# Conditioning columns from small fp32 products with the summed rows as stationary operand, in place of broadcast sums and their diagonal

## The chip, the cores and the metric

The kernel runs on one core of one Trainium2 chip. Its engines are TensorE (PE in the profile; its weight loads are shown apart as PEld), VectorE (DVE), ScalarE (ACT), GpSimd (POOL) and SyncE (SP, which here issues nearly all DMAs). The metric is the time of one execution in device microseconds, the median of three runs.

## The reference, cut to what matters

One layer for 256 tokens of width 2048 (D), with a conditioning vector `c` for the whole sequence. Each of three sublayers is modulated by columns of `ada`, and closed by a gate and a layer norm:

```python
ada = (silu(c) @ w_ada + b_ada)[:, None, :]          # 2048 -> 9 * 2048
sh1, sc1, g1, sh2, sc2, g2, sh3, sc3, g3 = split(ada, 9, axis=-1)
h = swiglu(layernorm(x) * (1 + sc1) + sh1, ffn1_w_in, ffn1_w_out)       # width 5632
x = layernorm(ALPHA * x + 0.5 * (1 + g1) * h, ln1_g, ln1_b)
h = token_mixer(layernorm(x) * (1 + sc2) + sh2, ..., w_in, ..., w_out)  # 8 FoX heads, 4 mLSTM heads
x = layernorm(ALPHA * x + (1 + g2) * h, ln2_g, ln2_b)
h = swiglu(layernorm(x) * (1 + sc3) + sh3, ffn2_w_in, ffn2_w_out)
x = layernorm(ALPHA * x + 0.5 * (1 + g3) * h, ln3_g, ln3_b)
```

The change concerns `sh2, sc2` (vectors 3 and 4 of the nine) and `sh3, sc3` (vectors 6 and 7): 2 x 2 x 2048 numbers.

## The kernel before, in words

**The products.** Every large product is made of three products in fp32r, a rounded fp32: `split` (L141) has ACT cast a tile to its rounded part `hi`, and DVE subtract that to get the rest `lo`; `mm3` (L368 to L371) then adds hi by hi, lo by hi and hi by lo into one accumulator of 128 x 256 or 128 x 512. One TensorE instruction is one such product with a stationary operand of 128 x 128. The weights arrive in DMAs of 1 MB, issued by SP at L344 into the three `raw` buffers; their halves are split into six `hi` and six `lo` buffers, so at most three loads are ahead of their use, and a load waits for its `raw` buffer.

**The stages**, in the order of the program: layer norm of `x`; FFN1 into the hidden rows (`gu_f`, L369 to L371), FFN1 out (`o_f`); a norm; the mixer's input products (`b_fv`, `b_mv`: values of the two kinds of heads, and others), the heads, and its output product (`o_mx`, from the weights `raw_mxo`, and the head outputs `yhi`, `ylo`); a norm; FFN2 in (`gu_f`) and out (`o_f`); the last norm.

**The conditioning.** `silu(c)` stands in `csil`, one column for each of 16 blocks of 128 rows of `w_ada`. `ada_acc` (L153) has DVE multiply a block of 128 rows by its column and add it to `acc`, 128 x 1024: sixteen such steps leave in `acc` a sum over blocks, and what is still to be summed is the 128 partitions. Each step is fed by a DMA of 512 KB on the SP queue (L179), into two `araw` buffers; so such a DMA waits for the accumulation two steps before, and whatever stands behind it on the SP queue waits too. `ada_gate` (L194) makes a gate, `ada_pair(v, js)` (L173) makes shift and scale together as columns: 512 features of vector `v` and 512 of `v+1` for each block `j`. In the text below a block is called 3_0 to 3_3 or 6_0 to 6_3 after its `v` and `j`; the eight blocks fill `scsh[:, v:v+2, 4j:4j+4]`, with feature 128q+p of the block in partition p and column q.

To sum over partitions, `ada_pair` before the change splits each 512-wide half of `acc` into `ahi` and `alo` and multiplies both by a stationary matrix of ones (`onesr`, in the trace `trir`): the sum `bc`, 128 x 512, then has every feature in every partition. DVE multiplies it by the identity (`dg`, L188) and reduces each 128 columns (L190), which leaves the diagonals: the columns wanted. Another DVE step adds the bias (L192).

**What sets the order.** The conditioning runs beside the big products as a generator, `ada_queue` (L218): gate of vector 2, blocks 3_0 to 3_3, 6_0 and 6_1, gate 5, blocks 6_2 and 6_3, gate 8. At fixed places of the program `pump(rate)` (L229) adds a rate (1.25 to 0.6 steps) to what is owed, and advances the generator by whole steps. A `yield PAUSE` ends the pump at once, with the debt kept: it gives the engines time between two dependent steps, and the generator makes the steps owed at the next pump. Within this, the framework's scheduler places the instructions on each engine, by their dependences and the buffers. `need` (L239) drains the generator to a point. Small sums use the PSUM pool of three `aux` buffers. Small tiles of the conditioning share the pool `ap` with one buffer per tag: `acc`, `ahi`, `alo`.

**A form that both kernels have.** For vectors 0 and 1, `first_columns` (L708) already makes columns with plain fp32 products: stationary `acc[:, v, qs]` of 128 x 128, moving `ones[:, 0:1]`, one result column (L716, tiles `cp` and `cq`).

Of the kernel before, what the change touches and what calls it, by code (L numbers as in the profile page):

```python
# [7 lines left out]
F32 = mybir.dt.float32  # L8
F32R = mybir.dt.float32r
AF = mybir.ActivationFunctionType  # L10
ALU = mybir.AluOpType
AX = mybir.AxisListType
PSUM = bass.MemoryType.PSUM

P = 128
T = 256
D = 2048
KD = D // P
# [14 lines left out]
def layer_kernel(  # L33
# [8 lines left out]
    V, S, G_, PE, SP = nc.vector, nc.scalar, nc.gpsimd, nc.tensor, nc.sync  # L42
# [16 lines left out]
    ap = ctx.enter_context(tc.tile_pool(name="ap", bufs=1))  # L59
# [7 lines left out]
    def aux_tile(name):  # L67
        return pa.tile([P, 512], F32, tag="aux", name=name)


    ident = cst.tile([P, P], F32, name="ident")
    G_.memset(ident, 0.0)
    G_.affine_select(out=ident, in_=ident, compare_op=ALU.not_equal, fill=1.0, base=0,
                     pattern=[[-1, P]], channel_multiplier=1)
    tri = ap.tile([P, 2 * P], F32, tag="ahi", name="tri")
    G_.memset(tri, 1.0)
    G_.affine_select(out=tri[:, :P], in_=tri[:, :P], compare_op=ALU.is_ge, fill=0.0, base=0,
                     pattern=[[1, P]], channel_multiplier=-1)
# [3 lines left out]
    ones, onesr = triu1[:, P:], trir[:, P:]  # L82


    crow = ap.tile([KD, P], F32, tag="alo", name="crow")
    SP.dma_start(crow, c[0].rearrange("(k p) -> k p", p=P))
    res = cst.tile([P, 2, D], F32, name="res")
    for a in range(2):
# [10 lines left out]
    G_.memset(mhalf, -0.5)  # L99

    def load_bcol():
        brow = ap.tile([72, 2, P], F32, tag="ahi", name="brow")
        SP.dma_start(brow, b_ada[0].rearrange("(h r p) -> r h p", h=2, p=P))
        bps = aux_tile("bps")
        for i in range(2):
            PE.transpose(bps[:, i * 72:(i + 1) * 72], brow[:, i, :], ident[:72, :72])
        V.tensor_copy(bcol.rearrange("p v k -> p (v k)"), bps[:, :144])
        for v in (1, 4, 7):
            V.tensor_scalar_add(bcol[:, v, :], bcol[:, v, :], 1.0)
# [31 lines left out]
    def split(src, hi, lo):  # L141
        S.copy(hi, src)  # L142
        return V.tensor_tensor(out=lo, in0=src, in1=hi.bitcast(F32), op=ALU.subtract)  # L143
# [15 lines left out]


    def ada_split(acc, tag):
        ahi = ap.tile([P, 512], F32R, tag="ahi", name=f"ahi{tag}")
        alo = ap.tile([P, 512], F32R, tag="alo", name=f"alo{tag}")
        split(acc, ahi, alo)
        return ahi, alo

    def ada_sum(parts, tag):
        bc = aux_tile(f"bc{tag}")
        for i in range(2):
            PE.matmul(bc, onesr, parts[i], start=i == 0, stop=i == 1)  # L170
        return bc

    def ada_pair(v, js):  # L173
        for j in js:
            src = pair_cols(v, j)
            acc = ap.tile([P, 2, 512], F32, tag="acc", name=f"acc{v}_{j}")
            for k in range(KD):
                raw = ap.tile([P, 2, 512], F32, tag="araw", bufs=2, name=f"ar{v}_{j}_{k}")
                SP.dma_start(raw, src[k * P:(k + 1) * P])  # L179
                ada_acc(acc, raw, k)  # L180
                yield
            for i in range(2):
                parts = ada_split(acc[:, i, :], f"{v}_{j}_{i}")
                for _ in range(2):
                    yield PAUSE
                bc = ada_sum(parts, f"{v}_{j}_{i}")
                dg = ap.tile([P, 4, P], F32, tag="alo", name=f"dg{v}_{j}_{i}")
                V.tensor_tensor(out=dg, in0=bc.rearrange("p (a b) -> p a b", b=P),  # L188
                                in1=ident.unsqueeze(1).to_broadcast([P, 4, P]), op=ALU.mult)
                V.tensor_reduce(out=scsh[:, v + i, j * 4:(j + 1) * 4], in_=dg, axis=AX.X, op=ALU.add)  # L190
            cs = scsh[:, v:v + 2, j * 4:(j + 1) * 4]
            V.tensor_tensor(out=cs, in0=cs, in1=bcol[:, v:v + 2, j * 4:(j + 1) * 4], op=ALU.add)  # L192

    def ada_gate(v, s):  # L194
        for j in range(2):
# [20 lines left out]
    PAUSE = 1  # L216
# [1260 lines left out]
```

## Time and profile before

| | us |
|---|---|
| median of three runs | 1932.42 (1932.11 to 1934.88) |
| profiled execution | 1936.38 |
| its span in the trace | 1934.7 |
| busy in the span: PE | 1895.6 (98%), 13085 instructions |
| PEld | 1722.5 (89%) |
| DVE | 1485.6 (77%) |
| ACT | 954.6 (49%) |
| POOL | 56.3 (3%) |
| bytes moved by DMA | 510.90 MB, mean 264 GB/s |
| granted TensorE clock, mean | 0.994 |

The profile is one execution; the span runs from its first to its last recorded instruction, and the run's own time is 1.7 us above it. A busy share of 98% is an average over stages: where an engine with such a share is never idle, every instruction added to it lengthens the run, while in a stage where it waits, the instruction that releases it counts. The profile's view by windows gives busy times stage by stage, the view of waits says in which stretch an engine stood idle and which instruction of which other engine ended that.

### The profile page before, as it was taken

The page shows a single profiled execution, that of the slowest core. Times are in us where ns is not written, and L with a number is a line of the kernel's source. Part 1 is how long each engine was busy: PE and PEld are TensorE (multiplying, and loading weights), DVE is VectorE, ACT ScalarE, POOL GpSimd, SP SyncE. Part 2 cuts the span into 40 slices and gives each one's busy share as a digit, 9 for nine tenths or more (in the row PEclk, how much of TensorE's full clock was granted, in tenths as well). Part 3 has the DMA queues.
Part 4 walks back from the last instruction along what each step waited for, and adds up shares of the span by engine and source line. Part 5 has one row for each costly group of instructions (what it writes and reads, how often), then busy time and mean ns, then how long its engine had stood idle before and what let it go on. Part 6 is the DMA issues. An engine that isn't in the chain of part 4 may idle for free.

```text
span 1934.7 us, 32285 instructions
## 1 busy us (share of the span) xinstructions
PE 1895.6 (98%) x13085; PEld 1722.5 (89%) x13085; DVE 1485.6 (77%) x1838; ACT 954.6 (49%) x1352; POOL 56.3 (3%) x82
## 2 busy tenths in 40 slices
PE   6999999999999999999999999999999999999997
PEld 3999999999988888698998786999999999988886
DVE  5779989777889898888888789777766665555776
ACT  3554454443454555845755545555444444444552
POOL 1111100000000000100000000000000000000000
PEclk8999999999999999999999999999999999999999
DMA  9978969899998786498888884997776776655552
GB/s 352 372 260 317 324 222 318 296 309 312 304 337 311 264 302 222 155 325 297 274 293 285 278 289 173 300 307 247 253 252 227 261 238 196 238 185 188 194 196 87
DMA packets 295709, 510.90 MB, mean 264 GB/s; under 512 B 10850, under 2 KB 158722, under 8 KB 294536
## 3 DMA queue, kind: packets, MB, share of 16 engines
q1 hardware_dynamic: 287784, 480.53, 73.3%
q0 software_dynamic: 7776, 28.32, 4.2%
q8 instruction: 102, 1.67, 0.3%
q14 instruction: 47, 0.39, 0.1%
HBM read 506.71 MB, written 2.10 MB: 263 GB/s over the span
## 4 chain that ended last, share of the span: by engine, by line
PE 78%; issue 11%; DMA 6%; DVE 3%; ACT 1%; POOL 0%; SPq 0%; DVEq 0%; ACTq 0%; POOLq 0%
PE gu_f L369 8%; PE gu_f L371 8%; PE gu_f L370 8%; PE o_f L369 8%; PE o_f L371 8%; PE o_f L370 8%; PE s L369 4%; PE s L371 4%; PE s L370 4%; DMA ar<-in_w_ada_dram 3%; PE fh L369 2%; PE fh L371 2%; PE fh L370 2%; PE fs L369 1%; PE fs L370 1%
## 5 line engine op out<-in xcount | busy, mean ns | idle before, releaser
L157 DVE SCALAR_TENSOR_TENSOR acc<-ar,csil,acc 128x1024 f32<-128x1024 f32 x242 | 308.0, 1274 | 84.4 <-DMA ar<-in_w_ada_dram 82.8
L369 PE MATMUL s<-xhi_f,hi_s 128*128 128x256 f32 x768 | 213.2, 278 | 1.1 <-ACT hT1a L825 1.1
L370 PE MATMUL s<-xlo_f,hi_s 128*128 128x256 f32 x768 | 213.1, 277 | 0.0
L371 PE MATMUL s<-xhi_f,lo_s 128*128 128x256 f32 x768 | 212.8, 277 | 0.0
L371 PE MATMUL gu_f<-xhi_f,lo_f2i 128*128 128x256 f32 x768 | 212.0, 276 | 0.0
L369 PE MATMUL gu_f<-xhi_f,hi_f2i 128*128 128x256 f32 x768 | 212.0, 276 | 0.0
L370 PE MATMUL gu_f<-xlo_f,hi_f2i 128*128 128x256 f32 x768 | 212.0, 276 | 0.0
L143 DVE TENSOR_TENSOR lo_f2i<-raw_f2i,hi_f2i 128x1024 fp32r<-128x1024 f32 x96 | 117.5, 1224 | 88.3 <-ACT hi_f2i L142 88.2
L371 PE MATMUL gu_f<-xhi_f,lo_f1i 128*128 128x256 f32 x640 | 176.7, 276 | 0.0
L369 PE MATMUL gu_f<-xhi_f,hi_f1i 128*128 128x256 f32 x640 | 176.7, 276 | 0.0
L370 PE MATMUL gu_f<-xlo_f,hi_f1i 128*128 128x256 f32 x640 | 176.7, 276 | 0.0
L142 ACT CAST hi_f2i<-raw_f2i 128x1024 fp32r<-128x1024 f32 x96 | 100.8, 1050 | 135.1 <-PE gu_f L370 124.3
L142 ACT CAST hi_s<-raw_s 128x1024 fp32r<-128x1024 f32 x96 | 100.3, 1052 | 130.1 <-PE s L370 83.7
L369 PEld LDWEIGHTS s<-xhi_f,hi_s 128*128 128x128 f32 x768 | 144.7, 189 | 1.3 <-ACT hT1a L825 1.3
L370 PEld LDWEIGHTS s<-xlo_f,hi_s 128*128 128x128 f32 x768 | 144.9, 189 | 0.2 <-DVE xlo_f L300 0.2
L371 PEld LDWEIGHTS s<-xhi_f,lo_s 128*128 128x128 f32 x768 | 144.9, 189 | 0.0
L370 PEld LDWEIGHTS gu_f<-xlo_f,hi_f2i 128*128 128x128 f32 x768 | 144.1, 188 | 0.2
L369 PEld LDWEIGHTS gu_f<-xhi_f,hi_f2i 128*128 128x128 f32 x768 | 144.1, 188 | 0.2
L371 PEld LDWEIGHTS gu_f<-xhi_f,lo_f2i 128*128 128x128 f32 x768 | 144.1, 188 | 0.0
L143 DVE TENSOR_TENSOR lo_f2o<-raw_f2o,hi_f2o 128x1024 fp32r<-128x1024 f32 x88 | 107.8, 1225 | 44.9 <-ACT hi_f2o L142 44.8
L143 DVE TENSOR_TENSOR lo_s<-raw_s,hi_s 128x1024 fp32r<-128x1024 f32 x96 | 115.8, 1223 | 29.0 <-ACT hi_s L142 29.0
L369 PE MATMUL o_f<-hi_f2o,hh 128*128 128x512 f32 x344 | 135.2, 393 | 0.0
(502 smaller groups left out, 5383.9 us busy)
## 6 DMA issues: line engine op xcount, KB each, us to landing
ar<-in_w_ada_dram SPq DMA_DIRECT2D x227, 512.0 KB, 5.6
raw_f2i<-in_ffn_w_in_dram SPq DMA_DIRECT2D x48, 1024.0 KB, 5.2
raw_s<-in_ffn_w_in_dram SPq DMA_DIRECT2D x47, 1024.0 KB, 7.4
raw_f1o<-in_ffn_w_out_dram SPq DMA_DIRECT2D x44, 1024.0 KB, 6.7
raw_f2o<-in_ffn_w_out_dram SPq DMA_DIRECT2D x44, 1024.0 KB, 5.0
raw_f1i<-in_ffn_w_in_dram SPq DMA_DIRECT2D x40, 1024.0 KB, 7.8
ar<-in_w_ada_dram POOLq DMA_DIRECT2D x48, 512.0 KB, 6.9
raw_mxo<-in_w_out_dram SPq DMA_DIRECT2D x16, 1024.0 KB, 6.3
```

The lines of the kernel that those rows point to most:

```text
L142: S.copy(hi, src)
L143: return V.tensor_tensor(out=lo, in0=src, in1=hi.bitcast(F32), op=ALU.subtract)
L157: V.scalar_tensor_tensor(out=acc, in0=raw, scalar=csil[:, k:k + 1], in1=acc, op0=ALU.mult, op1=ALU.add)
L369: PE.matmul(o, ah, bh, start=start, stop=False)
L370: PE.matmul(o, ah, bl, start=False, stop=False)
L371: PE.matmul(o, al, bh, start=False, stop=stop)
```

## The change

Each block's `acc` is copied once by ACT into `rows`, 128 x 1024. After two pauses, eight products in plain fp32 take 128 columns each of `rows` as the stationary operand and one column of ones as the moving one; each leaves the sums of 128 features as one column of `cp` in PSUM, 128 x 8 for the block. One DVE step adds the bias and writes `scsh`. The two splits, the four products with the matrix of ones, the multiplication by the identity, the two reductions and two of the four pauses are gone. In the gates, which keep the matrix of ones, the split parts now lie in one tile `as`; `tri`, `brow` and `crow`, used at the start, take other tags.

```diff
--- before.py
+++ after.py
@@ -72,7 +72,7 @@
     G_.memset(ident, 0.0)
     G_.affine_select(out=ident, in_=ident, compare_op=ALU.not_equal, fill=1.0, base=0,
                      pattern=[[-1, P]], channel_multiplier=1)
-    tri = ap.tile([P, 2 * P], F32, tag="ahi", name="tri")
+    tri = ap.tile([P, 2 * P], F32, tag="as", name="tri")
     G_.memset(tri, 1.0)
     G_.affine_select(out=tri[:, :P], in_=tri[:, :P], compare_op=ALU.is_ge, fill=0.0, base=0,
                      pattern=[[1, P]], channel_multiplier=-1)
@@ -82,7 +82,7 @@
     ones, onesr = triu1[:, P:], trir[:, P:]
 
 
-    crow = ap.tile([KD, P], F32, tag="alo", name="crow")
+    crow = ap.tile([KD, P], F32, tag="acc", name="crow")
     SP.dma_start(crow, c[0].rearrange("(k p) -> k p", p=P))
     res = cst.tile([P, 2, D], F32, name="res")
     for a in range(2):
@@ -99,7 +99,7 @@
     G_.memset(mhalf, -0.5)
 
     def load_bcol():
-        brow = ap.tile([72, 2, P], F32, tag="ahi", name="brow")
+        brow = ap.tile([72, 2, P], F32, tag="as", name="brow")
         SP.dma_start(brow, b_ada[0].rearrange("(h r p) -> r h p", h=2, p=P))
         bps = aux_tile("bps")
         for i in range(2):
@@ -159,10 +159,9 @@
 
 
     def ada_split(acc, tag):
-        ahi = ap.tile([P, 512], F32R, tag="ahi", name=f"ahi{tag}")
-        alo = ap.tile([P, 512], F32R, tag="alo", name=f"alo{tag}")
-        split(acc, ahi, alo)
-        return ahi, alo
+        parts = ap.tile([P, 2, 512], F32R, tag="as", name=f"as{tag}")
+        split(acc, parts[:, 0, :], parts[:, 1, :])
+        return parts[:, 0, :], parts[:, 1, :]
 
     def ada_sum(parts, tag):
         bc = aux_tile(f"bc{tag}")
@@ -179,17 +178,16 @@
                 SP.dma_start(raw, src[k * P:(k + 1) * P])
                 ada_acc(acc, raw, k)
                 yield
+            rows = ap.tile([P, 2, 512], F32, tag="as", name=f"rows{v}_{j}")
+            S.copy(rows, acc)
+            for _ in range(2):
+                yield PAUSE
+            cp = aux_tile(f"cc{v}_{j}")[:, :8].rearrange("p (v k) -> p v k", v=2)
             for i in range(2):
-                parts = ada_split(acc[:, i, :], f"{v}_{j}_{i}")
-                for _ in range(2):
-                    yield PAUSE
-                bc = ada_sum(parts, f"{v}_{j}_{i}")
-                dg = ap.tile([P, 4, P], F32, tag="alo", name=f"dg{v}_{j}_{i}")
-                V.tensor_tensor(out=dg, in0=bc.rearrange("p (a b) -> p a b", b=P),
-                                in1=ident.unsqueeze(1).to_broadcast([P, 4, P]), op=ALU.mult)
-                V.tensor_reduce(out=scsh[:, v + i, j * 4:(j + 1) * 4], in_=dg, axis=AX.X, op=ALU.add)
-            cs = scsh[:, v:v + 2, j * 4:(j + 1) * 4]
-            V.tensor_tensor(out=cs, in0=cs, in1=bcol[:, v:v + 2, j * 4:(j + 1) * 4], op=ALU.add)
+                for q in range(4):
+                    PE.matmul(cp[:, i, q:q + 1], rows[:, i, q * P:(q + 1) * P], ones[:, 0:1], start=True, stop=True)
+            V.tensor_tensor(out=scsh[:, v:v + 2, j * 4:(j + 1) * 4], in0=cp, in1=bcol[:, v:v + 2, j * 4:(j + 1) * 4],
+                            op=ALU.add)
 
     def ada_gate(v, s):
         for j in range(2):
```

The line numbers of the changed kernel are lower by two behind the first edit, so L369 to L371 of before are L367 to L369 there.

**On PE**, in FFN1 in, around block 3_0. The `gu_f` rows are the large products; `bc` are the products with the matrix of ones (`trir`), the second half's a hundred instructions after the first's. Before:

```order
L371 MATMUL gu_f120_1_5700<-xhi_f1_124,lo_f1i20_0_11_5790 128x256
L170 MATMUL bc3_0_0_5817<-ahi3_0_0_5689,trir_87 128x512
L170 MATMUL bc3_0_0_5817<-alo3_0_0_5690,trir_87 128x512
L369 MATMUL gu_f120_0_5699<-xhi_f1_124,hi_f1i20_1_00_5829 128x256
...
L371 MATMUL gu_f120_1_5700<-xhi_f1_124,lo_f1i20_1_11_5916 128x256
L170 MATMUL bc3_0_1_5943<-ahi3_0_1_5823,trir_87 128x512
L170 MATMUL bc3_0_1_5943<-alo3_0_1_5824,trir_87 128x512
L369 MATMUL gu_f121_0_5975<-xhi_f1_124,hi_f1i21_0_00_5979 128x256
```

Now, with `rows` as the stationary operand:

```order
L368 MATMUL gu_f120_1_5694<-xlo_f1_125,hi_f1i20_0_11_5783 128x256
L369 MATMUL gu_f120_1_5694<-xhi_f1_124,lo_f1i20_0_11_5784 128x256
L188 MATMUL cc3_0_5811<-trir_87,rows3_0_5685 128x1 x8
L367 MATMUL gu_f120_0_5693<-xhi_f1_124,hi_f1i20_1_00_5836 128x256
L368 MATMUL gu_f120_0_5693<-xlo_f1_125,hi_f1i20_1_00_5836 128x256
```

Two pairs at two places have become eight in one place, between two large products as before.

**On SP**, from the mixer's products for the values (`raw_mv512_3` is the last weight load of one column range, `raw_mv0` and `raw_m0a`, `raw_m0b` follow; `ar6_1_k` is step k of block 6_1). Before:

```order
L344 DMA raw_mv512_3_9271<-in_w_in_dram 128x4x520
L344 DMA raw_mv0_0_9351<-in_w_in_dram 128x4x512
L344 DMA raw_mv0_1_9401<-in_w_in_dram 128x4x512
L179 DMA ar6_1_0_9492<-in_w_ada_dram 128x2x512
L344 DMA raw_mv0_2_9450<-in_w_in_dram 128x4x512
L179 DMA ar6_1_1_9495<-in_w_ada_dram 128x2x512
L344 DMA raw_mv0_3_9526<-in_w_in_dram 128x4x512
L344 DMA raw_m0a_0_9572<-in_w_in_dram 128x8x256
L344 DMA raw_m0a_1_9633<-in_w_in_dram 128x8x256
L179 DMA ar6_1_2_9498<-in_w_ada_dram 128x2x512
L344 DMA raw_m0b_0_9694<-in_w_in_dram 128x8x256
L179 DMA ar6_1_3_9501<-in_w_ada_dram 128x2x512
```

Now:

```order
L342 DMA raw_mv512_3_9252<-in_w_in_dram 128x4x520
L178 DMA ar6_1_0_9240<-in_w_ada_dram 128x2x512
L178 DMA ar6_1_1_9243<-in_w_ada_dram 128x2x512
L342 DMA raw_mv0_0_9335<-in_w_in_dram 128x4x512
L178 DMA ar6_1_2_9246<-in_w_ada_dram 128x2x512
L178 DMA ar6_1_3_9249<-in_w_ada_dram 128x2x512
L342 DMA raw_mv0_1_9381<-in_w_in_dram 128x4x512
L178 DMA ar6_1_4_9318<-in_w_ada_dram 128x2x512
L178 DMA ar6_1_5_9369<-in_w_ada_dram 128x2x512
L342 DMA raw_mv0_2_9433<-in_w_in_dram 128x4x512
L178 DMA ar6_1_6_9372<-in_w_ada_dram 128x2x512
L178 DMA ar6_1_7_9415<-in_w_ada_dram 128x2x512
```

The pauses of block 6_0 stood here: up to `raw_m0a_1` two steps of the conditioning went between the loads, and now there are two behind each load.

**On SP**, at the end of the mixer's output product, where `raw_mxo1536_*` are the last weight loads and `ar6_2_k`, `ar6_3_k` steps of the blocks 6_2 and 6_3. Before:

```order
L344 DMA raw_mxo1536_1_12272<-in_w_out_dram 128x4x512
L179 DMA ar6_2_10_12101<-in_w_ada_dram 128x2x512
L179 DMA ar6_2_11_12142<-in_w_ada_dram 128x2x512
L179 DMA ar6_2_12_12181<-in_w_ada_dram 128x2x512
L179 DMA ar6_2_13_12184<-in_w_ada_dram 128x2x512
L344 DMA raw_mxo1536_2_12282<-in_w_out_dram 128x4x512
L179 DMA ar6_2_14_12223<-in_w_ada_dram 128x2x512
L179 DMA ar6_2_15_12262<-in_w_ada_dram 128x2x512
L344 DMA raw_mxo1536_3_12294<-in_w_out_dram 128x4x512
L179 DMA ar6_3_0_13025<-in_w_ada_dram 128x2x512
L344 DMA raw_mxo1536_0_12306<-in_w_out_dram 128x4x512
L179 DMA ar6_3_1_13028<-in_w_ada_dram 128x2x512
```

Now:

```order
L342 DMA raw_mxo1024_0_12169<-in_w_out_dram 128x4x512
L178 DMA ar6_2_12_12007<-in_w_ada_dram 128x2x512
L178 DMA ar6_2_13_12048<-in_w_ada_dram 128x2x512
L342 DMA raw_mxo1536_1_12222<-in_w_out_dram 128x4x512
L178 DMA ar6_2_14_12089<-in_w_ada_dram 128x2x512
L178 DMA ar6_2_15_12128<-in_w_ada_dram 128x2x512
L178 DMA ar6_3_0_12636<-in_w_ada_dram 128x2x512
L178 DMA ar6_3_1_12639<-in_w_ada_dram 128x2x512
L342 DMA raw_mxo1536_2_12232<-in_w_out_dram 128x4x512
L342 DMA raw_mxo1536_3_12244<-in_w_out_dram 128x4x512
L342 DMA raw_mxo1536_0_12256<-in_w_out_dram 128x4x512
```

The steps have moved ahead of the loads: `raw_mxo1536_2` was behind step 13 of block 6_2 and is now behind step 1 of block 6_3, and the two loads after it have no step between them.

## The prediction

> **What bounds the kernel now.** I read the page first, its busy times and its chain of waits.
>
> ```profile
> PE 1895.6 (98%) x13085; PEld 1722.5 (89%) x13085; DVE 1485.6 (77%) x1838; ACT 954.6 (49%) x1352; POOL 56.3 (3%) x82
> ...
> PE 78%; issue 11%; DMA 6%; DVE 3%; ACT 1%; POOL 0%; SPq 0%; DVEq 0%; ACTq 0%; POOLq 0%
> ```
>
> PE is busy nearly throughout, but the chain ends in other hands for some per cent. So the second view is the one by windows, cut where the eight blocks stand: 3_0 to 3_3 between 500 and 770, 6_0 and 6_1 between 865 and 1000, 6_2 and 6_3 between 1160 and 1312. Its columns are busy us (instructions) of PE, PEld, DVE, ACT and POOL, then clock, DMA share and GB/s.
>
> ```profile
> 75.00:775.00 700.00, 699.98 (x5083) 654.91 (x5082) 591.29 (x665) 334.48 (x417) 27.76 (x38) 1.00 0.86 295
> 825.00:925.00 100.00, 100.00 (x723) 93.80 (x722) 81.29 (x119) 51.30 (x87) 0.00 (x0) 1.00 0.92 311
> 925.00:1100.00 175.00, 167.17 (x1239) 156.79 (x1238) 145.64 (x229) 105.91 (x201) 1.65 (x1) 0.99 0.87 289
> 1100.00:1175.00 75.00, 73.55 (x323) 58.65 (x322) 61.24 (x70) 30.23 (x39) 0.59 (x1) 1.00 0.82 280
> 1205.00:1300.00 95.00, 95.00 (x786) 92.78 (x785) 71.45 (x78) 54.93 (x91) 0.00 (x0) 1.00 0.91 300
> 1325.00:1900.00 575.00, 575.00 (x4061) 533.89 (x4060) 378.87 (x411) 270.19 (x322) 0.00 (x0) 1.00 0.66 221
> ```
>
> In 75 to 775, in 825 to 925, in 1205 to 1300 and in 1325 to 1900 PE is busy for the whole window at full clock: there only the number and the length of PE's own instructions count, and a faster DVE or ACT is worth nothing. Idle time of PE that the change could reach is in the mixer alone, 925 to 1175. The third view is that of PE's waits over 825 to 1175, with us in total, times and longest:
>
> ```profile
> PE ptp L1093 <- ACT s L1088: 2.5, 2, 1.4
> PE sps L1201 <- DVE dm L1207: 1.9, 1, 1.9
> PE ptp L1093 <- DVE gate L211: 1.6, 1, 1.6
> PE o_mx L370 <- DVE lo_mxo L143: 1.2, 2, 0.7
> PE o_mx L369 <- ACT yhi L142: 1.0, 1, 1.0
> PE ytp L1249 <- DVE yl L1256: 0.5, 1, 0.5
> PE o_mx L371 <- DVE ylo L143: 0.3, 1, 0.3
> ```
>
> They sum to 9.0 us. That is all that could be won by order or by relief of DVE; everything else of this change is a count of PE's passes.
>
> **What PE loses and gains.** Removed are 4 products of 128x512 a block. Their pace stands in the timeline of PE at block 3_0 (start, length, then the instruction); lengths overlap, so I count from start to start:
>
> ```profile
> 499.68 0.39 PE L170 MATMUL bc<-ahi,trir 128*128 128x512 f32 x1
> 499.91 0.39 PE L170 MATMUL bc<-alo,trir 128*128 128x512 f32 x1
> 500.14 0.28 PE L369 MATMUL gu_f<-xhi_f,hi_f1i 128*128 128x256 f32 x1
> ```
>
> From 499.68 to 500.14 two take 0.46 us, 0.23 each: 0.92 a block, 7.4 for eight blocks. That they lie between large products on a busy engine means the whole of it comes off.
>
> Added are 8 products a block, plain fp32, stationary 128x128, moving one column. The kernel has such products: those of the first columns, L716, amid large products in the same way.
>
> ```profile
> 170.95 0.28 PE L371 MATMUL s<-xhi_f,lo_s 128*128 128x256 f32 x1
> 171.06 0.50 PE L716 MATMUL cp<-trir,gate 128*128 128x1 f32 x4
> 171.43 0.58 PE L716 MATMUL cq<-trir,gate 128*128 128x1 f32 x4
> 171.87 0.36 PE L369 MATMUL s<-xhi_f,hi_s 128*128 128x256 f32 x1
> 172.07 0.28 PE L370 MATMUL s<-xlo_f,hi_s 128*128 128x256 f32 x1
> ...
> 238.97 0.28 PE L371 MATMUL s<-xhi_f,lo_s 128*128 128x256 f32 x1
> 239.27 0.61 PE L716 MATMUL cp<-trir,acc 128*128 128x1 f32 x4
> 239.74 0.58 PE L716 MATMUL cq<-trir,acc 128*128 128x1 f32 x4
> 240.19 0.36 PE L369 MATMUL s<-xhi_f,hi_s 128*128 128x256 f32 x1
> ```
>
> A row `x4` here is two products: the code issues two for a column, and each is recorded as two passes. So four passes cost 0.37 (171.06 to 171.43) or 0.44 (171.43 to 171.87, up to the large product behind), about 0.11 a pass, though a pass moves one column only; a large product of 256 columns starts as often (170.95 to 171.06). Sixteen passes a block: 0.37 for the first four and 0.44 for each other, 1.69. The large product behind them takes 0.20 to its successor (171.87 to 172.07) where 0.12 is usual: 0.08 more. Together 1.77 a block, 14.2 for eight. The lower bound is 16 passes at 0.37 for four, with the slower successor: 1.56, 12.5. The upper one is the second sample, 0.92 for eight passes, twice, plus 0.08: 1.92, 15.4. Net on PE: 14.2 - 7.4 = **+6.8 us**, between +5.1 and +8.0. No engine waits in its favour: four blocks stand in 75 to 775 and one in 1205 to 1312, where PE has no gap to take them in.
>
> [...]
>
> **What DVE and ACT are spared.** Their prices, min/median/max ns of one and the count:
>
> ```profile
> L142 ACT CAST ahi<-acc x28: 612/620/658, 335.0 to 1626.1; 128x512 fp32r<-128x512 f32 x28
> L143 DVE TENSOR_TENSOR alo<-acc,ahi x28: 683/685/701, 339.7 to 1627.8; 128x512 fp32r<-128x512 f32 x28
> ...
> L188 DVE TENSOR_TENSOR dg<-bc,ident x16: 682/690/692, 500.3 to 1308.9; 128x512 f32<-128x512 f32 x16
> L190 DVE TENSOR_REDUCE scsh<-dg x16: 665/681/686, 502.1 to 1310.2; 128x4 f32<-128x512 f32 x16
> ...
> L142 ACT CAST hi_s<-raw_s 128x1024 fp32r<-128x1024 f32 x96 | 100.3, 1052 | 130.1 <-PE s L370 83.7
> ```
>
> DVE loses two subtractions, two products with the identity and two reductions a block: 2 x (0.685 + 0.690 + 0.681) = 4.1, 32.9 in all. ACT has two casts of 0.62 replaced by one copy of 1024 columns, about 1.05 by the cast of that size: 0.2 less a block. Both lie beside a busy PE, so I enter 0 for them outside the mixer; without that cover, were DVE the bound, they would be worth the 32.9. The bias add stays, now from PSUM.
>
> The added wait is that of the copy for the last accumulation step; behind it on ACT stand casts of weights, for which DVE's subtraction and then PE wait. Before, a cast of the same `acc` stood in the same place and waited for the same step, so I enter 0; the copy holds ACT 0.4 longer than one cast, and where the weights are many microseconds ahead nothing comes of it.
>
> **What moves in the mixer.** Two pauses fewer a block let the conditioning run ahead. The first place is the start of the output product. There, on DVE and on ACT:
>
> ```profile
> 1086.65 1.28 DVE L157 SCALAR_TENSOR_TENSOR acc<-ar,csil,acc 128x1024 f32<-128x1024 f32 x1 [2.66 <-DMA ar<-in_w_ada_dram]
> ...
> 1087.97 0.62 ACT L142 CAST ahi<-acc 128x512 fp32r<-128x512 f32 x1 [2.31 <-DVE acc L157]
> ...
> 1089.46 1.15 ACT L142 CAST yhi<-yF 128x512 fp32r<-128x512 f32 x2
> ```
>
> ACT stands 2.31 us for gate 5's last step, which itself waits for its DMA, and the casts of `yhi` stand behind it in ACT's order; the waits for `yhi` and `ylo` (1.0 and 0.3) come from there. In the change that last step comes earlier in DVE's order, ahead of the subtraction of the first output weights, so its split is out of the way: **-1.3**, at worst 0.
>
> The second is the end of that product, where SP's rows are:
>
> ```profile
> 1157.13 0.37 SPq L344 DMA_DIRECT2D raw_mxo<-in_w_out_dram  x1
> 1161.69 0.37 SPq L179 DMA_DIRECT2D ar<-in_w_ada_dram  x1
> 1164.70 0.37 SPq L344 DMA_DIRECT2D raw_mxo<-in_w_out_dram  x1
> 1165.12 0.50 SPq L179 DMA_DIRECT2D ar<-in_w_ada_dram  x1
> ```
>
> A weight load stands behind two steps of the conditioning whose `araw` buffers come free slowly, so it goes out 7.6 us after the one ahead of it, and PE waits 1.2 us for `lo_mxo`. In the change the same obstacle, now steps 14 and 15 of 6_2 and 0 and 1 of 6_3, stands ahead of the load before, and the two last have nothing ahead of them. The ends are -1.2 (it vanishes) and +2.5 (four steps in a row where there were two, so about twice the present loss, 2 x 1.2, on top); I enter 0, the loss kept at another load, since the obstacle is of the same kind.
>
> The third is behind `raw_mv512_3`, about 875 to 905. Two steps of 0.5 MB now go with each load of 1 MB where the pauses of 6_0 had left a rest. At 311 GB/s with a DMA share of 0.92, full use would be 338 GB/s, and 2 MB take 6.2 us. One load is worth 24 products of 0.23 on PE, 5.5 us. So each such load loses 0.6 to 0.7 us of its lead over its use; six loads in a row lose about 4. If the lead is gone at their start PE waits up to 3.6; with 2 or 3 us of lead, 1 to 2; with more, nothing. I enter **+1.5**. The waits for `ptp`, `sps` and `ytp` are chains within the heads, and I leave them: 0.
>
> **The sum**: 6.8 - 1.3 + 0 + 1.5 = +7.0. The profiled execution took 1936.38, its span 1934.7; the terms are differences, so I set them on the median, 1932.42, which is 4 us lower: **1939.4 us**, +0.36%. Its own range, from +2.6 (5.1 - 1.3 - 1.2) to +10.5 (8.0 + 1.5 + 1.0), is 1935 to 1943.
>
> **The rivals.**
>
> *Relief of DVE and an earlier conditioning clear the mixer's waits* (not slower). Five of the seven rows of waits end at DVE, or at ACT behind DVE; four blocks fall in or by the mixer. If all 9.0 go, 6.8 - 9.0 = -2.2: 1930.2; with the lower price of the passes -3.9: 1928.5. It decides from the point where more than 6.8 us of waiting goes. Against it: 925 to 1100 has DVE busy 145.64 of 175, and by the order only one of those waits loses its cause.
>
> *The lead is used up* (slower than I say). In 875 to 905 PE waits the full 3.6, and the late load at the end of the output product costs 2.5 more, with no gain elsewhere: 6.8 + 3.6 + 2.5 = 12.9, 1945.3. For it: a DMA share of 0.92 there already. Against it: lost lead can be won back after, and shows then only once.
>
> *The small products cost next to nothing*: they slip beside their neighbours' loads of the stationary operand. Then PE is spared 7.4 and pays nearly nothing: -7.4 + 0.2 for the moves, 1925. [...] Against it, the quoted passes of 0.11, which also stood between large products and cost their full time.
>
> *The change doesn't do what it says* would be products that need another form than L716 had; the order lists the same form, so I give it no chance of its own.
>
> **How the numbers follow.** The forecast 0.57, the relief 0.21, the lead used up 0.18, products for nothing 0.04. A measurement here tells some 0.2% from no change, 3.9 us: 1928.6 to 1936.3. Slower: 0.18 from the lead and 0.48 of the forecast's 0.57, whose lower end lies under 1936.3; so 0.66. Within: the 0.09 left of the forecast and 0.13 of the relief; 0.22. Faster: 0.08 of the relief and 0.04; 0.12. The range goes to the relief at its middle and to the lead used up, 1930 to 1945, leaving out the last 0.08 and 0.04 below and some 0.07 above.
>
> **What would show it right or wrong.** At L188, sixteen passes between two large products, first to next 1.6 to 1.9 us; 0.5 or less would favour the third rival. PE's rows of 75 to 775 and 1325 to 1900 with no idle in them, as before, and the last large product of FFN1 in four blocks' net later, 3.4 us. The wait for `yhi` gone; a new one on `hi_mv` or `lo_mv` between 875 and 905; one on `lo_mxo` of about 1 us. If the sum of PE's waits over the mixer falls under 3 us, the relief was underrated and I am wrong.

## The result, and the profile after

| | before | changed |
|---|---|---|
| median, us | 1933.62 (1930.50 to 1936.71, six runs) | 1945.07 (1941.38 to 1949.25, six runs) |
| profiled execution, us | 1936.38 | 1944.59 |
| its span, us | 1934.7 | 1942.9 |

The ratio is 1.0059, with a 95% interval of 1.0045 to 1.0074: 11.4 us, or 8.7 to 14.3. The forecast was 1939.4, and its range ended at 1945.0, so the median lies just above it. A second measurement of the same kernel, with the experiments below, gave 1.0074 (1.0053 to 1.0095). In all that follows 0.001 of the ratio is 1.9 us. The two profiled executions differ by 8.2 us, less than the medians: the one of before lies near the top of what that kernel's runs span. So the traces are used for where the time goes, and the ratios for how much it is.

From the page of the changed kernel, busy times:

```profile
PE 1901.8 (98%) x13181; PEld 1731.3 (89%) x13181; DVE 1459.8 (75%) x1790; ACT 955.5 (49%) x1344; POOL 56.5 (3%) x82
```

DVE is busy 26 us less (1485.6 before) and the run is longer: that relief bought nothing. PE is busy 6.2 us more.

The view by windows of the changed kernel (busy us and instructions of PE, PEld, DVE, ACT, POOL; clock, DMA share, GB/s):

```profile
75.00:775.00 700.00, 700.00 (x5110) 656.39 (x5109) 574.37 (x636) 332.70 (x410) 27.82 (x38) 1.00 0.86 294
825.00:925.00 100.00, 95.22 (x663) 87.39 (x662) 77.75 (x111) 43.50 (x78) 0.00 (x0) 1.00 0.90 303
925.00:1100.00 175.00, 170.66 (x1305) 162.34 (x1304) 141.79 (x224) 112.28 (x205) 1.65 (x1) 0.99 0.87 290
1100.00:1175.00 75.00, 74.04 (x340) 60.42 (x339) 62.70 (x72) 33.71 (x44) 0.59 (x1) 1.00 0.87 293
1205.00:1300.00 95.00, 93.55 (x736) 87.64 (x735) 70.56 (x73) 56.58 (x94) 0.00 (x0) 1.00 0.91 296
1325.00:1900.00 575.00, 574.93 (x4070) 533.95 (x4069) 371.48 (x406) 270.73 (x326) 0.00 (x0) 1.00 0.65 216
```

Two windows in which PE had no gap before now have one: 825 to 925 (95.22 of 100, 60 instructions fewer) and 1205 to 1300 (93.55 of 95, 50 fewer). In 925 to 1100 PE waits less than before, 4.3 us against 7.8.

PE's waits in the changed kernel, 825 to 1185, with us in total, times and longest:

```profile
PE sps L1199 <- DVE dm L1205: 3.0, 1, 3.0
PE b_mv L368 <- DVE lo_mv L143: 2.3, 2, 1.4
PE pr_m L367 <- ACT hi_m0a L142: 1.2, 1, 1.2
PE pr_m L369 <- DVE lo_m0a L143: 1.0, 2, 0.8
PE o_mx L367 <- DVE res L433: 0.9, 1, 0.9
PE pr_m L369 <- DVE lo_m1a L143: 0.8, 1, 0.8
PE pr_m L369 <- DVE lo_m0b L143: 0.3, 1, 0.3
PE ptp L1091 <- ACT s L1086: 0.3, 1, 0.3
PE ptp L1091 <- DVE gate L209: 0.2, 1, 0.2
```

The waits for `yhi`, `ylo` and `lo_mxo` are gone, those for `ptp` nearly (0.5 against 4.1); new are one for `res`, 0.9 us, and those for the split weights `mv`, `m0a`, `m0b` and `m1a`, 5.6 us. These are the halves of weight loads that came too late. Outside this window the same view has `PE fh L369 <- DVE lo_fh`, 1.3 us, likewise new.

How far one trace is behind the other, place by place, I read from the starts of the same product in each. The table gives the start before, and the delay against it in the changed kernel (first and second measurement) and in two of the experiments below:

| first product of | before, us | changed | again | four pauses | two of eight, four pauses |
|---|---|---|---|---|---|
| `cp3`, ahead of all blocks | 239.3 | -1.7 | -0.8 | -1.3 | -0.8 |
| the norm behind FFN1 | 778.5 | +1.4 | +2.2 | +1.9 | -3.1 |
| the values `b_mv`, second part | 877.6 | +4.6 | +4.3 | +2.4 | -3.0 |
| `gb0`, the first mLSTM head | 941.0 | +12.4 | +8.9 | +4.4 | -0.9 |
| `ptp2`, in the output product | 1109.6 | +5.8 | +1.0 | +1.2 | -0.8 |
| last output weights, first use | 1162.7 | +8.5 | +7.2 | +1.2 | -0.8 |
| last output weights, second part | 1176.6 | +5.8 | +4.4 | +0.8 | -2.2 |
| `fh3`, FFN2 in | 1227.3 | +5.5 | +4.8 | +1.2 | -1.3 |
| `fh9` | 1294.0 | +9.1 | +7.8 | +1.7 | -1.4 |
| late in FFN2 in | 1636.9 | +8.2 | +6.8 | +2.4 | -2.0 |

FFN1 costs 3.0 to 3.2 us for four blocks in each kernel with all the small products. Behind it the differences hold two things: what the order costs, and the blocks' own products, which lie at other places in the two kernels. A block's sixteen passes stand in one place and make a step of 1.70 us in the delay; a pair of products with the matrix of ones, of which the kernel before has two a block, makes one of 0.47 us, and for three of the four blocks of the mixer these pairs come behind a mark that the passes are ahead of. Gate 5 keeps its pairs, but they move too. (With four pauses the two halves of a block stand where the pairs stood, 0.34 us net each.) With these steps taken out, the table gives for the order alone, in us:

| from, to | changed | again | four pauses |
|---|---|---|---|
| 778 to 941, weights for the values and the first head | +8.5 | +4.2 | +1.8 |
| 941 to 1110, the heads and the start of the output product | -6.1 | -7.4 | -3.9 |
| 1110 to 1177, the rest of the output product | -1.2 | +2.2 | -0.4 |
| 1227 to 1294, first weights of FFN2 in | +2.4 | +1.8 | +0.2 |

These are differences of single traces. Behind 1294 nothing is given back: the 0.9 us by which the delay shrinks up to 1637 are block 6_3's own products in the kernel before.

### The profile page after: what moved, and what is told of

Same layout as the page of the kernel before. It is cut to its first block, busy times and chain, and to the rows that moved or that the text cites. A ratio compares the mean times of both kernels' runs of the same rounds, so it can differ in the third digit from the quotient of the medians.

```text
span 1942.9 us, 32428 instructions
## 1 busy us (share of the span) xinstructions
PE 1901.8 (98%) x13181; PEld 1731.3 (89%) x13181; DVE 1459.8 (75%) x1790; ACT 955.5 (49%) x1344; POOL 56.5 (3%) x82
## 4 chain that ended last, share of the span: by engine, by line
PE 85%; DMA 8%; DVE 4%; ACT 1%; issue 1%; SPq 0%; POOL 0%; DVEq 0%; ACTq 0%; POOLq 0%
PE gu_f L367 8%; PE gu_f L369 8%; PE gu_f L368 8%; PE o_f L367 8%; PE o_f L369 8%; PE o_f L368 8%; PE s L367 4%; PE s L368 4%; PE s L369 4%; DMA ar<-in_w_ada_dram 3%; DVE acc L157 2%; PE fs L368 1%; PE fs L367 1%; PE fs L369 1%; PE fh L369 1%; PE fh L367 1%
## 5 line engine op out<-in xcount | busy, mean ns | idle before, releaser
L367 PE MATMUL s<-xhi_f,hi_s 128*128 128x256 f32 x768 | 213.4, 279 | 0.4 <-ACT hT1a L823 0.4
L369 PE MATMUL s<-xhi_f,lo_s 128*128 128x256 f32 x768 | 213.0, 277 | 0.0
L369 PE MATMUL gu_f<-xhi_f,lo_f2i 128*128 128x256 f32 x768 | 212.0, 276 | 0.0
L367 PE MATMUL gu_f<-xhi_f,hi_f2i 128*128 128x256 f32 x768 | 212.0, 276 | 0.0
L367 PE MATMUL gu_f<-xhi_f,hi_f1i 128*128 128x256 f32 x640 | 176.8, 276 | 0.0
L369 PE MATMUL gu_f<-xhi_f,lo_f1i 128*128 128x256 f32 x640 | 176.7, 276 | 0.0
L367 PEld LDWEIGHTS s<-xhi_f,hi_s 128*128 128x128 f32 x768 | 144.9, 189 | 0.6 <-ACT hT1a L823 0.6
L369 PEld LDWEIGHTS s<-xhi_f,lo_s 128*128 128x128 f32 x768 | 145.0, 189 | 0.0
L367 PEld LDWEIGHTS gu_f<-xhi_f,hi_f2i 128*128 128x128 f32 x768 | 144.1, 188 | 0.2
L369 PEld LDWEIGHTS gu_f<-xhi_f,lo_f2i 128*128 128x128 f32 x768 | 144.1, 188 | 0.0
L367 PE MATMUL o_f<-hi_f2o,hh 128*128 128x512 f32 x344 | 135.2, 393 | 0.0
```

The lines of the kernel that those rows point to most:

```text
L367: PE.matmul(o, ah, bh, start=start, stop=False)
L369: PE.matmul(o, al, bh, start=False, stop=stop)
```

## The experiments

Each ran beside the kernel before on the same chip, in five rounds. Theory A keeps the prediction's 6.8 us for the passes and puts what is left of the loss on the order, which the prediction had not; its rivals name one of the two.

**Undoing the order alone.** The pauses of before are put back: two ahead of each half's products.

```diff
-            for _ in range(2):
-                yield PAUSE
             cp = aux_tile(...)
             for i in range(2):
+                for _ in range(2):
+                    yield PAUSE
                 for q in range(4):
                     PE.matmul(...)
```

> The changed kernel with the pauses of before: two ahead of each half's four small products, four in a block. The DMA order on SP behind raw_mv512_3 is then again that of before (two steps of block 6_1 over six weight loads). Theory A (two causes: the passes cost 6.8 us, and the rest comes from the conditioning running ahead at 6_0, where the weights' lead is used up): 6.8 us over the kernel before, ratio 1.0035 (1.0026 to 1.0041), no PE wait on weights between 860 and 945. Theory B (the passes cost all of it): as the changed kernel, ratio 1.0059. Theory C (the order costs all of it, the passes nothing): ratio 1.000.

Measured: 1.0039 (1.0024 to 1.0053), 7.5 us. Theory A's 6.8 lies in the interval, 1.0059 and 1.000 do not. PE's waits on weights between 860 and 945 shrank to one of 1.0 us (`lo_m1b`), not to none.

**The other half alone: the large products at the pace of the change.**

```diff
                 parts = ada_split(acc[:, i, :], ...)
-                for _ in range(2):
+                for _ in range(1):
                     yield PAUSE
```

> The kernel before with one pause for each half in place of two, two in a block: the large products with ones, the diagonal and the reductions stay, while the DMA order on SP becomes that of the changed kernel (two steps of the conditioning behind each weight load from raw_mv512_3 on). Theory A: the order's share alone, about 11.4 - 6.8 = 4.6 us over before, ratio 1.0024, with PE waiting for lo_mv and for the m0a weights; more if DVE's heavier load there delays the splits further. Theory B: ratio 1.000. Theory C: 1.0059.

Measured: 1.0068 (1.0041 to 1.0094), 13 us where 4.6 were expected. The trace shows that this edit did more than was meant. PE's waits in it:

```profile
PE bc L170 <- DVE alo L143: 4.7, 4, 3.2
...
PE bc L170 <- ACT ahi L142: 2.9, 1, 2.9
```

With one pause between a split and its product, PE reaches the product before the split is done, 7.6 us in all. So this run doesn't measure the order alone; it shows what a pause is for.

**Doubling the passes.** All eight products are issued twice in a row.

```diff
-            for i in range(2):
+            for i in (0, 1, 0, 1):
                 for q in range(4):
                     PE.matmul(...)
```

> The changed kernel with the eight small products of each block issued twice into the same columns: 128 more passes on PE, no other work. Theory A: 128 passes at 0.11 us, 14.2 us over the changed kernel, 25.6 over before, ratio 1.0132. Theory B: the passes cost 11.4 + 7.4 = 18.8 us for 128, so 30 over before, ratio 1.0156. Theory C: as the changed kernel, 1.0059.

Measured: 1.0190 (1.0161 to 1.0220), 37 us, more than any theory had. The mean granted clock fell to 0.987 (0.982 to 0.989 in five runs), from 0.995. The windows of this kernel around its first block say where, the clock being the third number from the end:

```profile
500.00:505.00 5.00, 5.00 (x30) 5.00 (x30) 3.67 (x5) 0.15 (x1) 0.00 (x0) 0.63 0.96 298
505.00:510.00 5.00, 5.00 (x33) 5.00 (x32) 2.73 (x4) 1.05 (x1) 0.00 (x0) 0.69 0.87 278
```

And its timeline of PE there:

```profile
499.02 4.74 PE L188 MATMUL cc<-trir,rows 128*128 128x1 f32 x32
503.63 0.56 PE L367 MATMUL gu_f<-xhi_f,hi_f1i 128*128 128x256 f32 x1
...
504.42 0.42 PE L367 MATMUL gu_f<-xhi_f,hi_f1i 128*128 128x256 f32 x1
504.63 0.42 PE L368 MATMUL gu_f<-xlo_f,hi_f1i 128*128 128x256 f32 x1
...
508.20 0.28 PE L367 MATMUL gu_f<-xhi_f,hi_f1i 128*128 128x256 f32 x1
508.31 0.28 PE L368 MATMUL gu_f<-xlo_f,hi_f1i 128*128 128x256 f32 x1
```

The 32 passes take 4.61 us (499.02 to 503.63), where 32 at 0.111 would take 3.55, and the large products behind them start every 0.21 us until 508, where 0.11 is usual: PE runs at about half its pace for some 5 us. At or behind each of the eight rows of this trace the clock stands at half for 3.4 or 6.8 us, though PE is busy in the records.

**The same passes in four groups of eight.**

```diff
-            for _ in range(2):
-                yield PAUSE
             cp = aux_tile(...)
-            for i in range(2):
+            for i in (0, 1, 0, 1):
+                yield PAUSE
                 for q in range(4):
                     PE.matmul(...)
```

> The small products of each block twice, as in the run with 32 passes in a row, but in four groups of eight passes (0.9 us each) with one pause ahead of each; the order on SP is near that of before. If the low clock in that run came from the length of the row (32 passes, 3.5 us), it is gone here: clock about 0.995, time 7 + 14.2 = 21 us over before, ratio 1.011. If the low clock follows the number of passes whatever their grouping, or the passes are simply dearer than 0.11: clock about 0.987, and 7 + 23.7 = 31 us over before, ratio 1.016.

Measured: 1.0109 (1.0091 to 1.0126), 21 us, as expected of a clock that depends on the length of the row; the interval excludes 1.016. The clock was 0.993 to 0.994, a little under the 0.995 expected, and the trace shows where. At blocks 3_3 and 6_3 `need` drained the generator, which skips the pauses, so that the groups ran together; between 60 and 1900 us the clock fell behind these two rows and nowhere else:

```profile
762.96 2.73 PE L187 MATMUL cc<-trir,rows 128*128 128x1 f32 x24
1317.82 3.63 PE L187 MATMUL cc<-trir,rows 128*128 128x1 f32 x32
```

```profile
766.40:769.80 3.40, 3.40 (x10) 2.65 (x9) 1.23 (x2) 0.00 (x0) 0.00 (x0) 0.51 0.32 39
1322.80:1326.20 3.40, 3.40 (x10) 2.66 (x9) 0.06 (x2) 0.66 (x2) 0.00 (x0) 0.50 0.62 204
```

So the price of a pass in groups of eight is confirmed by a doubling, and what the longer row adds is the clock: of 37 - 21 = 16 us, a mean clock of 0.987 or 0.988 in place of 0.995 alone accounts for some 14 to 16, so the order's share can't be told from this pair. With sixteen passes in a row, as in the change, the windows above show a clock of 1.00 in 75 to 775.

**A rest at one block.** Four pauses at block 6_0, two at all others; then the same at block 6_2; then at both.

```diff
-            for _ in range(2):
+            for _ in range(4 if (v, j) == (6, 0) else 2):
                 yield PAUSE
```

> The changed kernel with four pauses at block 6_0 alone, two at the other seven. Theory A: most of the order's share goes, since the rest at 6_0 is what lets the weights regain their lead: 7 to 9 us over before, ratio 1.0035 to 1.0047, and PE's waits on lo_mv, hi_m0a and lo_m0a (4.5 us in the changed kernel) mostly gone. Theory B: 1.0059. If the order matters elsewhere in the mixer, also near 1.0059, but with those waits gone.

Measured: 1.0046 (1.0031 to 1.0062). PE has no wait at all between 860 and 945, as expected, and from 778 to 941 the order's loss, counted as in the table, is 0.3 us in place of 8.5 and 4.2. So the missing rest at 6_0 is the cause of the loss there.

> The changed kernel with four pauses at block 6_2 alone. On SP, block 6_3's steps then start behind five loads of FFN2's first weights (fh) instead of behind two. Theory A, now with two places for the order's share (the values' weights at 875 to 945, mostly given back in the heads, and the first fh weights at 1227 to 1294, given back nowhere): the second place goes, some 3 us less than the changed kernel (1.0059 and 1.0074 in two measurements): 1.0045 to 1.0055, no PE wait on lo_fh, the waits on lo_mv or m0a weights still there. Rival (the order's loss is all at the first place): as the changed kernel.

Measured: 1.0049 (1.0030 to 1.0068). The time is where theory A had it; but PE still waited 1.2 us for the `fh` weights, which was not expected, and the order's loss from 1227 to 1294 is still there, 1.7 us, only later, from 1277 on.

> The changed kernel with four pauses at blocks 6_0 and 6_2, two at the other six. Theory A: both places go, and what is left are the passes: 6.8 us, ratio 1.0035 (1.0025 to 1.0042), as with four pauses everywhere. Rival (a third place, or all the earlier conditioning, matters): above 1.0050.

Measured: 1.0034 (1.0019 to 1.0049), theory A's number, again with a wait for `fh` weights, of 1.6 us, and a loss of 3.7 us from 1227 to 1294, of which 1.7 are a stretch of half clock (0.50 over 3.4 us from 1280.8). The three intervals overlap one another and that of the changed kernel. They agree with the first place; the second was not taken away by a rest at 6_2, only moved, so what the order costs there isn't settled by these runs.

**The changed kernel again, and six of eight products left out.** In the second and third kernel only the first column of each four is made, and copied to the other three; the third also has the four pauses of before.

```diff
-                for q in range(4):
+                for q in range(1):
                     PE.matmul(...)
-            V.tensor_tensor(out=..., in0=cp, ...)
+            V.tensor_tensor(out=..., in0=cp[:, :, 0:1].to_broadcast([P, 2, 4]), ...)
```

> The changed kernel, unaltered, on the same chip and beside the same runs of the kernel before as the three that follow. Theory A now has three parts: passes at 0.11 us (+6.8), weights' lead used up where the rest at 6_0 is gone (+3 to +5), and now and then a stretch of low TensorE clock behind a row of one-column passes (+0 to +3 in a run). Expected again 1.005 to 1.006 of before, 10 to 12 us over it, with a mean clock at or a little under that of before.

Measured: 1.0074 (1.0053 to 1.0095).

> The changed kernel with two of each block's eight small products, each result put into four columns; six products, and so three quarters of the columns, are left out. The order on SP stays that of the changed kernel. Theory A: four passes a block cost 0.44 + 0.08, net 0.52 - 0.92 = -0.40 a block, -3.2 in all, and the order's +3 to +5 stays: -0.2 to +1.8 us, ratio 0.9999 to 1.0009, with PE's waits on lo_mv and m0a weights still there. Rival (the order costs nothing, all of the loss is in the passes, 18.8 us for 128): 4.7 - 7.4 = -2.7, ratio 0.9986, without those waits.

Measured: 1.0020 (1.0008 to 1.0032), 3.9 us over before, with PE's waits still there:

```profile
PE b_mv L368 <- DVE lo_mv L143: 2.1, 3, 1.1
PE b_mv L367 <- ACT hi_mv L142: 1.0, 1, 1.0
PE pr_m L369 <- DVE lo_m0a L143: 0.8, 1, 0.8
```

> As the run ahead of this one (two of eight products, three quarters of the columns left out), with the four pauses of before. Theory A: the order's share is gone too: -3.2 us, ratio 0.9983, no wait on weights between 860 and 945. Rival (order costs nothing): as the run ahead of this one, difference under 1 us.

Measured: 0.9995 (0.9984 to 1.0006). The two intervals don't overlap, and the kernels differ by pauses alone: 0.0025, **4.8 us, is the price of the order** (2 to 8 by the two intervals). With nearly all passes gone the loss stays when the order stays, so the passes don't explain it all; with both gone it is gone. Both kernels came out some 2 us above their expected numbers, for which I have no shown cause.

**Cheaper passes.** `rows` is split into two bf16 parts, each column is two bf16 products, with the four pauses of before.

```diff
-            rows = ap.tile([P, 2, 512], F32, tag="as", ...)
-            S.copy(rows, acc)
+            rows = ap.tile([P, 2, 2, 512], BF16, tag="as", ...)
+            S.copy(rows[:, 0], acc)
+            V.tensor_tensor(out=rows[:, 1], in0=acc, in1=rows[:, 0], op=ALU.subtract)
...
+                    for h in range(2):
+                        PE.matmul(cp[:, i, q:q + 1], rows[:, h, i, q * P:(q + 1) * P], ones16, start=h == 0, stop=h == 1)
...
+    ones16 = cst.tile([P, 1], BF16, name="ones16")
+    G_.memset(ones16, 1.0)
```

> Four pauses as before everywhere; the summed rows are split into two bf16 parts (one ACT cast and one DVE subtraction of 128x1024 a block), and each column is two bf16 products of one pass each, sixteen passes a block as in the changed kernel, with stationary operands of half the width. If a pass costs the load of 128 columns whatever their type (0.11): 7 us over before, ratio 1.0035. If the load of 128 bf16 columns is much shorter, 0.03 to 0.06 a pass: 0.5 to 1.0 + 0.08 a block in place of 0.92, -2.7 to +1.3 us, ratio 0.9986 to 1.0007, the only version of this study that could beat the kernel before.

Measured: 1.0234 (1.0211 to 1.0257), 45 us, though the passes are as cheap as could be hoped. The timeline of PE around the first eight of them:

```profile
514.82 0.35 PE L193 MATMUL cc<-ones,rows 128*128 128x1 bf16 x8
515.03 0.36 PE L372 MATMUL gu_f<-xhi_f,hi_f1i 128*128 128x256 f32 x1
```

Eight passes take 0.21 us, 0.026 each, a quarter of the fp32 ones. The loss is not at the passes: against the kernel before, the starts of the same products fall behind by some 1.5 us every 40 us while FFN1 in and FFN2 in run (4%), by 1.2 us in FFN2 out (3%), and by only 2.5 us in all between 600 and 1200, where FFN1 out and the mixer lie. A window of 20 us in FFN2 in holds 172 large products:

```profile
1540.00:1560.00 20.00, 20.00 (x172) 20.00 (x172) 10.37 (x11) 7.99 (x10) 0.00 (x0) 1.00 0.69 234
```

In the kernel before such a window has 179, at the same clock:

```profile
1500.00:1520.00 20.00, 20.00 (x179) 20.00 (x178) 12.34 (x12) 8.88 (x10) 0.00 (x0) 1.00 0.84 277
```

So each large product of this stage has become 4% longer, and what this kernel has besides the passes is a constant of two bytes a partition, which moved everything allocated behind it.

**The same without the new constant.** The bf16 one is the upper half of a fp32 one in the matrix of ones.

```diff
-    ones16 = cst.tile([P, 1], BF16, name="ones16")
-    G_.memset(ones16, 1.0)
+    ones16 = trir.bitcast(BF16)[:, 2 * P + 1:2 * P + 2]
```

> As the run with two bf16 parts, but without the new tile: the column of bf16 ones is the upper half of a fp32 one in the matrix of ones that is there already, so no constant behind it moves. The run before showed the bf16 passes at 0.026 us each (eight in 0.21, and 0.09 more for the product behind them: 0.60 a block in two groups), and all large products 4% slower from the start. Theory A (the 2-byte tile shifted every later constant and with it the moving operands): the 4% are gone, the products cost 0.60 - 0.92 = -0.32 a block, -2.6 us, ratio 0.9987 (0.9977 to 0.9997). Rival (the bf16 products themselves slow down the others): again near 1.02.

Measured: 0.9992 (0.9981 to 1.0003), median 1932.45 against 1935.04 for before, run beside it. The 4% are gone:

```profile
1500.00:1520.00 20.00, 20.00 (x179) 20.00 (x178) 12.53 (x12) 7.92 (x9) 0.00 (x0) 1.00 0.77 264
```

This is the best version of the study. Its ratio lies 0.7 to 0.8% under that of the changed kernel (0.9992 against 1.0059 and 1.0074); against the kernel before the interval includes no change, and a gain of 2.6 us isn't shown. Its mean clock over twelve runs was 0.993, that of before 0.995.

## Why the prediction was wrong

**The bound, right but for two windows.** In 75 to 775 and in 1325 to 1900 PE has next to no gap, as said. In 825 to 925 and in 1205 to 1300, where only PE's own instructions were to count, it now has one of 4.8 and of 1.5 us: a stage without waits before the change isn't safe from what the change does to the queue. Neither DVE's relief of 26 us nor ACT's changed anything that the runs can tell.

**The passes, right, and to the size.** The timeline of PE in the changed kernel at block 3_0:

```profile
497.85 0.28 PE L369 MATMUL gu_f<-xhi_f,lo_f1i 128*128 128x256 f32 x1
497.96 1.84 PE L188 MATMUL cc<-trir,rows 128*128 128x1 f32 x16
499.66 0.36 PE L367 MATMUL gu_f<-xhi_f,hi_f1i 128*128 128x256 f32 x1
499.86 0.28 PE L368 MATMUL gu_f<-xlo_f,hi_f1i 128*128 128x256 f32 x1
```

From 497.96 to 499.66 are 1.70 us, and the product behind takes 0.20: 1.78 with its 0.08 too much, where 1.77 was said. The net of +6.8 stands against 7.5 (4.6 to 10.3) in the run with the order of before, and against 3.0 to 3.2 us for the four blocks of FFN1 in the table, where 3.4 was said. The rival of small products that cost next to nothing is out for fp32. The bf16 passes, at 0.026, come near it. On PEld the load of one such operand is recorded with 96 ns (median) in bf16 and with 192 in fp32; the passes follow each other by 26 and by some 110. That the load sets the pace of a pass, as one reading in the expectation of the bf16 run has it, isn't shown.

**The order's terms, wrong: this is the step that failed.** I had entered -1.3 + 0 + 1.5 = +0.2 us; the runs show +4.8. The forecast's own range had the same fault: its top took +1.5 and +1.0 for terms whose own upper bounds were 3.6 and 2.5. With these it is 8.0 + 3.6 + 2.5 = 14.1, or 1946.5, which holds the measured time. By its places:

- *Start of the output product, -1.3*: the waits for `yhi` and `ylo` are gone from both traces of the changed kernel, as said.
- *End of the output product, 0*: within its bounds, but by another wait. Without block 6_2's own passes, which fall here, the changed kernel gains 1.2 us from 1110 to 1177 in its first trace and loses 2.2 in the second; its bounds had been -1.2 and +2.5. PE's wait on `lo_mxo` is gone from both. The new one, for `res`, is 0.9 in the first and 2.2 in the second, where 3.4 us at half clock follow it (0.50 from 1145.5), 1.7 us more: that is most of the difference. A wait for `res` stands in all traces with two pauses; with four, only the one with doubled products has one, of 0.3 us. That the order makes it is likely, and wasn't tried by itself.
- *Behind `raw_mv512_3`, +1.5, at most 3.6*: mis-sized. SP's rows in the changed kernel:

```profile
868.01 2.17 SPq L178 DMA_DIRECT2D ar<-in_w_ada_dram  x2
870.24 0.46 SPq L342 DMA_DIRECT2D raw_mv<-in_w_in_dram  x1
...
881.26 2.70 SPq L178 DMA_DIRECT2D ar<-in_w_ada_dram  x2
884.01 0.46 SPq L342 DMA_DIRECT2D raw_mv<-in_w_in_dram  x1
888.15 3.29 SPq L178 DMA_DIRECT2D ar<-in_w_ada_dram  x2
891.50 0.47 SPq L342 DMA_DIRECT2D raw_mv<-in_w_in_dram  x1
...
902.34 4.53 SPq L178 DMA_DIRECT2D ar<-in_w_ada_dram  x2
906.92 0.74 SPq L342 DMA_DIRECT2D raw_m0a<-in_w_in_dram  x1
```

From 870.24 to 906.92 go five loads, 7.3 us each (6.8 in the second measurement, over six loads). I had priced a load with its two steps by bytes, 2 MB at 338 GB/s, 6.2 us. What sets the pace is the queue: a step's DMA stands on SP until one of two `araw` buffers is free, that is until an earlier step has landed and DVE has used it, and the weight load stands behind it. SP's own waits between 866 and 910 show it, first the two longest rows of the changed kernel, then the longest of before:

```profile
SPq L178 <- DMA ar<-in_w_ada_dram: 15.4, 9, 2.6
SPq L178 <- DVE acc L157: 12.7, 7, 2.3
```

```profile
SPq L344 <- DVE lo_mv L143: 17.6, 4, 6.9
```

In the changed kernel every wait of SP there is one ahead of a step; before, most of the time SP waited at a weight load for its `raw` buffer, with the loads ahead of their use. Against PE's 5.5 us a load, 1.3 to 1.8 us are lost on each, not 0.6, on six of them 8 to 11. The table of the order alone has 8.5 and 4.2 between 778 and 941; what lead took up the rest wasn't measured. Much of it came back in the heads, 6.1 and 7.4 us by 1110, which I hadn't entered. In the second trace 1.7 of it is a stretch of half clock that the heads of before have and it has not (0.50 over 3.4 us from 950.5). Of the rest, 3.9 came back with four pauses too, where there was little delay to absorb; so some 2 us are left that a stage in which PE waits for other engines can have absorbed.

- *A fourth place, not foreseen*: the first weights of FFN2 in. In the trace of before SP issues eight `fh` loads in one row ahead of the steps of block 6_3:

```profile
1205.05 28.86 SPq L344 DMA_DIRECT2D raw_fh<-in_ffn_w_in_dram  x8
```

In the changed kernel, where 6_2 ends earlier, its steps start behind two:

```profile
1218.04 1.69 SPq L178 DMA_DIRECT2D ar<-in_w_ada_dram  x2
1219.84 0.41 SPq L342 DMA_DIRECT2D raw_fh<-in_ffn_w_in_dram  x1
1224.48 2.70 SPq L178 DMA_DIRECT2D ar<-in_w_ada_dram  x2
1227.27 0.42 SPq L342 DMA_DIRECT2D raw_fh<-in_ffn_w_in_dram  x1
1231.50 2.70 SPq L178 DMA_DIRECT2D ar<-in_w_ada_dram  x2
1234.25 1.05 SPq L342 DMA_DIRECT2D raw_fh<-in_ffn_w_in_dram  x1
```

Again some 7.2 us a load (1219.84 to 1234.25, two loads), before any lead was built. It costs 2.4 and 1.8 us in the two traces of the changed kernel, and 0.2 in that with four pauses. Behind it PE has next to no idle time, and nothing comes back. I had looked for the moved steps in the mixer and stopped at its end. That two loads ahead, and not eight, is the reason is argued from the order: with five ahead, as the rest at 6_2 leaves it, the loss came later and was about as large.

**The rivals.** "The lead is used up" was the right one by its mechanism, at a chance of 0.18; its 1945.3 is met by 1945.07, but not by its own sum: it had 3.6 us behind `raw_mv512_3`, where more was lost and much of it given back, 2.5 at the end of the output product, where the traces differ, and nothing at the place in FFN2. That its number was met is luck. (By its own reading six, not five, of its seven rows of waits end at DVE or behind it; nothing hangs on that.) The relief of DVE, as a gain in time, is out: the waits of the mixer did fall, at `ptp`, `yhi` and `lo_mxo`, and new ones of the same sum came (10.0 us over 825 to 1185, by the rows above, against 9.0). With four pauses their sum is 6.4 in one trace and, with two of eight products, 10.0 in another, so what relief alone is worth isn't shown. 6.8 for the passes and 4.8 for the order are 11.6 us, the measured 11.4; with the order known only to 2 to 8, that they meet so closely is chance.

## What to carry to other kernels

On a busy TensorE a pass of an fp32 product cost 0.11 us here with one column moving, as often as a large product of 256 columns starts: count passes and their types before trading wide products for narrow ones. An edit that takes pauses or waits out of a side job also moves that job's DMAs in the queue it shares with the main one, so look for every stage into which it now runs, beyond the one it left, and price a queue by what its entries wait for (buffers, the engine that frees them) rather than by bytes alone: here a load took 7.3 us in it, where bytes gave 6.2. Of a delay ahead of the heads, where PE waits for other engines, some 2 us can have been absorbed here; of the 2.4 and 1.8 us lost at the first weights of FFN2, ahead of a stage in which PE is busy 574.93 of 575 us, nothing came back. And before a difference between two traces is put on waiting, take out the work that has merely moved past the mark.

## What the runs showed of the hardware that was not expected

- A row of 32 one-column fp32 passes brought the granted TensorE clock down to 0.63 over 5 us, with PE busy for all of the 5.00; one of 24, 2.6 us long, brought it to 0.51 over the 3.4 us at 766.4. Rows of sixteen, 1.7 us long, did so at none of the eight blocks in either trace of the changed kernel, nor did rows of eight. The stretches of half clock last 3.4 or 6.8 us. The row of 32 took 4.61 us where 32 passes at 0.111 would take 3.55, and the products behind it ran at 0.21 us in place of 0.11. Why a long row of such passes lowers the clock isn't shown.
- A constant of two bytes a partition ahead of the others made the products of FFN1 in and FFN2 in 4% slower (172 in place of 179 in 20 us), those of FFN1 out hardly (175 in place of 177 in 40 us), and taking it away undid that (179 again). Why it does so isn't shown.
- One-column bf16 passes took 0.026 us against 0.11 in fp32.
